# A decoder block on one Trainium2 core: three small pads shift the SBUF addresses of the matmul operands

## The chip, the core and the metric

The kernel runs on one core of one Trainium2 chip. The core has a matrix engine (TensorE: PE for the matmuls, PEld for the loads of their stationary operands), VectorE (DVE), ScalarE (ACT), GpSimd (POOL) and SyncE (SP), which here issues most of the DMAs. Tiles lie in the on-chip memory SBUF, which has 128 partitions; an address in this text is a byte address within a partition, the same in all of them. The metric is the device time of one execution in microseconds (us), the median of several.

## The reference

One layer of a decoder for 256 positions and 1024 channels, all float32:

```python
h = rmsnorm(x, ln1)
z = h @ w_in                      # q, k, v of three attentions, and three gates
o_a, o_b, o_c = moba_attention(..), forgetting_attention(..), sliding_window_sink_attention(..)
merged = sigmoid(ga) * (o_a @ w_pa) + sigmoid(gb) * (o_b @ w_pb) + sigmoid(gc) * (o_c @ w_pc)
x = x + merged @ w_o
h2 = rmsnorm(x, ln2)
u = causal_dwconv(h2 @ w_up, conv_w, conv_b)   # w_up: 1024 x 5632, three taps
a, b = split(u, 2)
return rmsnorm(x + (silu(a) * b) @ w_down, ln_f)   # w_down: 2816 x 1024
```

## The kernel before

**Numbers.** Every float32 product is made of three matmuls of a 4-byte type with fewer bits (float32r). Each operand is split into a high part and a rest: ScalarE copies the high part (`whi`, L110), VectorE subtracts it from the original (`wlo`, L117), and hi·hi, lo·hi and hi·lo are added up in PSUM. A matmul has a stationary operand of 128 x 128 and a moving operand of 128 partitions and up to 512 columns. Here both are read as 4-byte elements out of SBUF.

**Two kinds of product.** In a row product (`mm3`, L255 to L257) the activation is stationary and 512 columns of the weight move: the v and gate columns of `w_in`, the projections `w_pa`, `w_pb`, `w_pc` (`project`, activation `oT`), `w_o` (`wo_mm`, activation `mT` in the buffers named `hThi`, `hTlo`) and `w_down` (`down_mm`, activation `ah`, `al`). In a column product the weight is stationary and 256 positions of the activation move: the q and k columns of `w_in` (`qk_piece`, L406) and all of `w_up` (`up_mm`, L872). `w_up` has 44 pieces of 128 columns; each takes 24 matmuls (8 slices of the contraction, 3 parts each), 1056 in all. Its moving operand `h2T` lies in the buffers that the attention outputs had before, and so carries the names `oThi` and `oTlo` in the trace.

**Stages.** q, k, v, the attentions and the gates until about 151 us; the projections until 172 us; `w_o` until 198 us; then the channel mixer, 22 rounds of two `w_up` pieces and, in 18 of them, one `w_down` piece of 12 matmuls with 512 columns, until about 372 us; then the last four `w_down` pieces at once and the final norm.

**Weights.** `Weights` brings pieces of 512 KB through five `raw` buffers, splits them some pieces ahead of their use and hands out tiles of 4096 bytes a partition. Until `W.more` is set (L727) there are six `whi` and six `wlo` buffers in the pool `wpool`. From there on four more of each lie in the pool `ml`, and of every ten pieces in turn the first six take a buffer of `wpool`, the other four one of `ml` (`Weights.part`):

```python
if i >= first and (i - first) % (HL_BUFS + MORE_BUFS) >= HL_BUFS:
    return pool.tile([P, 1024], F32R, name=name, tag=name + "m", bufs=MORE_BUFS)
return self.pool.tile([P, 1024], F32R, name=name, tag=name, bufs=HL_BUFS)
```

**Addresses.** Pools lie one behind the other in SBUF, `const`, `wpool`, `act` and then, in the place that the attention's pool `attn` gives up, `ml`; inside a pool, tiles lie in the order in which they are first made. A tile that is made longer, or one that is made and never used, shifts all that follow it. All slices that matmuls read start at whole multiples of 256 bytes from the start of their tile, but for the v columns of `w_in` (780 floats to a piece). So the address of a tile modulo 256 is that of its slices.

Of the kernel before, what the change touches and what calls it, by code (L numbers as in the profile page):

```python
# [7 lines left out]
F32 = mybir.dt.float32  # L8
# [4 lines left out]
P = 128  # L13
# [127 lines left out]
def hybrid_kernel(ctx: ExitStack, tc: tile.TileContext, x, xT, ln_f, w_main, w_v1, w_v2, b_f, sinks,  # L141
# [4 lines left out]
    const = ctx.enter_context(tc.tile_pool(name="const", bufs=1))  # L146
    wpool = ctx.enter_context(tc.tile_pool(name="wpool", bufs=1))
    act = ctx.enter_context(tc.tile_pool(name="act", bufs=1))
# [36 lines left out]
    load_x(6, 8)  # L185
    W.load_to(4)
    cv = const.tile([P, 192], F32, name="cv")[:, :4 * 2 * NF + KD]
    ln2 = cv[:, 8 * NF:8 * NF + KD]
    W.load_to(6)
    for t in range(2):  # L190
# [68 lines left out]
    def small(shape, name, bufs=2):  # L259
        return act.tile([P] + shape, F32, name=name, tag=name, bufs=bufs)  # L260
# [269 lines left out]

    foxb = G[:, 1].rearrange("p t c -> p (t c)")[:, 0:4 * ROWS].rearrange("p (h c) -> p h c", h=4)
    lf, cum = small([8], "lf", 1), small([16], "cum", 1)[:, :8]

    def fox(logits):
        logits()
# [48 lines left out]


    oT = [act.tile([P, 8, S], F32R, name=n, tag=n, bufs=1) for n in ("oThi", "oTlo")]
    pair_state = {}

    def pair_of(p):
        if p < 2:  # L590
# [493 lines left out]
```

## Time and profile before

| what | us |
|---|---|
| median of 3 runs (394.5 to 395.8) | 395.03 |
| the profiled execution | 394.46 |
| its span, first to last instruction | 392.7 |
| PE busy | 382.7 |
| VectorE busy | 301.9 |
| ScalarE busy | 239.7 |

The profile is of one execution; 1.8 us of it lie outside the span. A matmul's own duration in the trace is no measure of what it costs, since matmuls overlap in the pipeline: one of 256 columns is listed with 0.28 us, and the next starts 0.11 to 0.12 us later. What counts is the time from one start to the next, called its step below. It is read from the starts of the first matmul of a run and of the first one behind it, divided by their number. The chain of waits gives the same: it lists runs of matmuls by length and number.

### The profile page before, as it was taken

Reading aid. Unit: us, or ns where it says so; the run is one execution under the profiler, and the core shown is the slowest. Engines: PE = TensorE matmul, PEld = TensorE weight load, DVE = VectorE, ACT = ScalarE, POOL = GpSimd, SP = SyncE. Lnnn points to the kernel's source line nnn. Section 1 sums busy time; section 2 is a strip of 40 time slices with the busy share of each in tenths; the row PEclk is TensorE's granted clock in tenths of the full one; section 3 lists DMA queues with packets and bytes.
Section 4 is the critical chain, followed back from the end, with each engine's and each line's share of the span. In section 5 each row is a group of like instructions: output and inputs, shape, how many; then the busy total and the mean of one; then the engine's idle time right before and its main releaser. Section 6 shows DMA issues by size and latency. Waiting matters only on the chain.

```text
span 392.7 us, 6636 instructions
## 1 busy us (share of the span) xinstructions
PE 382.7 (97%) x2464; PEld 346.9 (88%) x2464; DVE 301.9 (77%) x572; ACT 239.7 (61%) x431; POOL 15.3 (4%) x50
## 2 busy tenths in 40 slices
PE   7999999999999999999999999999999999999992
PEld 6899999888888888888899999999999999999982
DVE  4788998766777727967778999778887878888745
ACT  5875867657566696336587667456654656555433
POOL 4811000000000000000000000000000000000000
PEclk9999999999999999999999999999999999999998
DMA  7989764443543546443726667555565555463002
GB/s 195 402 308 344 271 213 164 161 141 116 173 120 103 165 150 221 154 160 118 259 107 221 205 214 236 198 187 189 164 213 174 204 169 204 166 212 107 2 1 108
DMA packets 21376, 70.88 MB, mean 180 GB/s; under 512 B 2504, under 2 KB 3413, under 8 KB 21344
## 3 DMA queue, kind: packets, MB, share of 16 engines
q1 hardware_dynamic: 20448, 68.05, 51.7%
q0 software_dynamic: 752, 2.18, 1.8%
q8 instruction: 19, 0.31, 0.3%
q10 hardware_dynamic: 144, 0.23, 0.2%
q14 instruction: 13, 0.11, 0.1%
HBM read 69.38 MB, written 1.07 MB: 179 GB/s over the span
## 4 chain that ended last, share of the span: by engine, by line
PE 96%; DMA 1%; DVE 1%; ACT 1%; SPq 1%; issue 0%; DVEq 0%
PE s L872 16%; PE acc L255 15%; PE acc L257 15%; PE acc L256 15%; PE pt L872 8%; PE o L872 8%; PE acc L406 7%; PE s L608 2%; PE pt L658 1%; DMA G<-in_xT 1%; PE pt L406 1%; PE o L406 1%; PE pt L661 1%; PE pt L645 1%; PE o L645 1%; PE s L313 0%
## 5 line engine op out<-in xcount | busy, mean ns | idle before, releaser
L117 DVE TENSOR_TENSOR wlo<-raw,whi 128x1024 fp32r<-128x1024 f32 (+4 forms) x131 | 150.5, 1162 | 14.1 <-ACT whi L110 13.8
L110 ACT ACTIVATE whi<-raw 128x1024 fp32r<-128x1024 f32 (+4 forms) x131 | 129.0, 1006 | 33.1 <-PE acc L256 21.7
L255 PE MATMUL acc<-whi,hThi 128*128 128x512 f32 (+2 forms) x160 | 62.4, 390 | 0.0
L257 PE MATMUL acc<-wlo,hThi 128*128 128x512 f32 (+2 forms) x160 | 60.1, 376 | 0.0
L256 PE MATMUL acc<-whi,hTlo 128*128 128x512 f32 (+2 forms) x160 | 59.9, 375 | 0.0
L872 PE MATMUL s<-oThi,whi 128*128 128x256 f32 x176 | 49.4, 281 | 0.0
L872 PE MATMUL s<-oThi,wlo 128*128 128x256 f32 x176 | 49.3, 281 | 0.0
L872 PE MATMUL s<-oTlo,whi 128*128 128x256 f32 x176 | 49.0, 281 | 0.0
L880 ACT ACTIVATE ya<-v,cv 128x256 f32<-128x256 f32 x22 | 13.3, 603 | 44.3 <-DVE v L877 44.3
L257 PEld LDWEIGHTS acc<-wlo,hThi 128*128 128x128 f32 x160 | 30.0, 188 | 5.4
L257 PE MATMUL acc<-wlo,ah 128*128 128x512 f32 (+1 forms) x88 | 34.2, 389 | 0.0
L255 PE MATMUL acc<-whi,ah 128*128 128x512 f32 (+1 forms) x88 | 34.1, 388 | 0.0
L256 PEld LDWEIGHTS acc<-whi,hTlo 128*128 128x128 f32 x160 | 30.2, 189 | 4.5 <-DVE hTlo L307 0.2
L256 PE MATMUL acc<-whi,al 128*128 128x512 f32 (+1 forms) x88 | 34.1, 388 | 0.0
L255 PEld LDWEIGHTS acc<-whi,hThi 128*128 128x128 f32 x160 | 30.1, 188 | 4.3
L872 PEld LDWEIGHTS s<-oThi,whi 128*128 128x128 f32 x176 | 33.1, 188 | 0.4
L872 PEld LDWEIGHTS s<-oThi,wlo 128*128 128x128 f32 x176 | 33.1, 188 | 0.4
L872 PEld LDWEIGHTS s<-oTlo,whi 128*128 128x128 f32 x176 | 32.9, 188 | 0.0
L872 PE MATMUL pt<-oThi,whi 128*128 128x256 f32 x88 | 24.8, 282 | 0.0
L872 PE MATMUL pt<-oThi,wlo 128*128 128x256 f32 x88 | 24.8, 282 | 0.0
L872 PE MATMUL o<-oThi,whi 128*128 128x256 f32 x88 | 24.8, 282 | 0.0
L872 PE MATMUL pt<-oTlo,whi 128*128 128x256 f32 x88 | 24.8, 282 | 0.0
(301 smaller groups left out, 801.5 us busy)
## 6 DMA issues: line engine op xcount, KB each, us to landing
raw<-in_w_main SPq DMA_DIRECT2D x115, 512.0 KB, 3.3
raw<-in_w_main SPq DMA_DIRECT2D x7, 256.0 KB, 6.1
raw<-in_w_v SPq DMA_DIRECT2D x4, 384.0 KB, 4.3
xt<-in_x SPq DMA_DIRECT2D x2, 512.0 KB, 6.9
G<-rowsd POOLq DMA_DIRECT2D x1, 1024.0 KB, 12.8
raw<-in_w_v SPq DMA_DIRECT2D x2, 390.0 KB, 6.6
G<-in_xT SPq DMA_DIRECT2D x3, 256.0 KB, 6.4
out_y<-xt SPq DMA_DIRECT2D x2, 288.0 KB, 2.2
```

Of the source, the lines that this page charges most:

```text
L110: self.nc.scalar.activation(self.parts[i][0][:, cs], self.raw[i][:, cs], AF.Copy)
L117: self.nc.vector.tensor_sub(lo[:, cs], self.raw[i][:, cs], hi[:, cs].bitcast(F32))
L255: nc.tensor.matmul(o, lh, rh, start=start, stop=False, **kw)
L256: nc.tensor.matmul(o, ll, rh, start=False, stop=False, **kw)
L257: nc.tensor.matmul(o, lh, rl, start=False, stop=stop, **kw)
L406: nc.tensor.matmul(o, w[:, kk, cs], hT[h][:, k, :], start=first, stop=last, skip_group_check=True)
L608: nc.tensor.matmul(sc, q[a][:, qi, qs], k[b][:, ki, :, 0:n], start=i == 0, stop=i == 2)
L645: nc.tensor.transpose(pts[e][:, i * P:(i + 1) * P], L[:, e, i * P:(i + 1) * P], ident)
L658: nc.tensor.matmul(o, v[a][:, vi, e, :], b[:, e, :], start=e == 0 and n == 0, stop=False, **kw)
L661: nc.tensor.matmul(o[:, P:S], v[2][:, vi, e, :], pT1[:, e, :], start=False, stop=e == 1, **kw)
L872: nc.tensor.matmul(u, w, h2T[h][:, k, :], start=k == 0 and i == 0, stop=k == KD - 1 and i == 2)
L880: nc.scalar.activation(y, v, AF.Identity, scale=w[2], bias=w[3])
```

## The change

Three tiles are added that nothing reads or writes, and a line that did nothing (`pair_state`) goes.

```diff
     cv = const.tile([P, 192], F32, name="cv")[:, :4 * 2 * NF + KD]
+    const.tile([P, 48], F32, name="pad0")
     ln2 = cv[:, 8 * NF:8 * NF + KD]
...
     lf, cum = small([8], "lf", 1), small([16], "cum", 1)[:, :8]
+    act.tile([P, 16], F32, name="pad1")
...
     oT = [act.tile([P, 8, S], F32R, name=n, tag=n, bufs=1) for n in ("oThi", "oTlo")]
-    pair_state = {}
+    act.tile([P, 32], F32, name="pad2")
```

The pads are 192, 64 and 128 bytes. All engines execute the same instructions in the same order with the same waits as before; only addresses differ. Modulo 256 they are, worked out from the order of the tiles (the distance is the moving operand's address less the stationary operand's, modulo 256):

| matmuls | number | columns | moving, stationary before | distance before | moving, stationary after | distance after |
|---|---|---|---|---|---|---|
| `w_up`, weight in `wpool` | 648 | 256 | 0, 128 | 128 | 0, 64 | 192 |
| `w_up`, weight in `ml` | 408 | 256 | 0, 192 | 64 | 0, 64 | 192 |
| `w_down`, weight in `wpool` | 159 | 512 | 128, 192 | 192 | 64, 64 | 0 |
| `w_down`, weight in `ml` | 93 | 512 | 192, 192 | 0 | 64, 64 | 0 |
| `w_down`, last columns, `wpool` | 18 | 256 | 128, 192 | 192 | 64, 64 | 0 |
| `w_down`, last columns, `ml` | 6 | 256 | 192, 192 | 0 | 64, 64 | 0 |
| `w_o`, weight in `ml` | 48 | 512 | 192, 128 | 64 | 64, 64 | 0 |
| `w_o`, weight in `wpool` | 48 | 512 | 128, 128 | 0 | 64, 64 | 0 |
| projections | 96 | 512 | 128, 0 | 128 | 64, 0 | 64 |
| q and k columns of `w_in` | 312 | 256 | 128, 128 | 0 | 64, 64 | 0 |
| gate and v columns of `w_in` | 384 | 260 to 512 | 128 to 160, 128 | 0 to 32 | 64 to 96, 64 | 0 to 32 |
| attention, products | 112 | 128 to 512 | 192, 192 | 0 | 64, 64 | 0 |
| attention, transposes | 48 | 128 | 128, 192 | 192 | 64, 64 | 0 |

## Rows read from the trace of the kernel before

**Rows 1.** The page: busy time, and the chain that ended last by engine and line
```profile
PE 382.7 (97%) x2464; PEld 346.9 (88%) x2464; DVE 301.9 (77%) x572; ACT 239.7 (61%) x431; POOL 15.3 (4%) x50
PE 96%; DMA 1%; DVE 1%; ACT 1%; SPq 1%; issue 0%; DVEq 0%
```

**Rows 2.** Waits of PE, whole span: who, for whom, us in total, times, longest
```profile
PE pt L406 <- ACT whi L110: 1.4, 2, 1.1
PE s L199 <- DVE warm L196: 1.1, 1, 1.1
PE pt L406 <- DVE wlo L117: 0.4, 2, 0.2
```

**Rows 3.** Chain in order of time, `w_up` alone: start, us, engine, PSUM tile, line, matmuls
```profile
198.59 1.42 PE s L872 x12
...
205.16 2.88 PE pt L872 x24
...
219.37 2.83 PE pt L872 x24
...
253.16 2.88 PE pt L872 x24
...
284.28 2.85 PE pt L872 x24
...
368.94 2.87 PE o L872 x24
```

**Rows 4.** Timeline of PE, last columns of `w_down`: start, us, engine, line, operation, out<-in
```profile
382.81 0.28 PE L255 MATMUL acc<-whi,ah 128*128 128x256 f32 x1
...
383.16 0.28 PE L255 MATMUL acc<-whi,ah 128*128 128x256 f32 x1
...
383.84 0.28 PE L255 MATMUL acc<-whi,ah 128*128 128x256 f32 x1
```

**Rows 5.** Chain in order of time: q and k columns, transposes, attention times v
```profile
52.29 6.47 PE acc L406 x54
58.76 0.33 PE pt L645 x3
...
63.92 0.71 PE pt L658 x6
...
179.72 0.87 PE s L313 x8
```

**Rows 6.** Timeline of PE: two `w_down` pieces, each with the first matmul behind it
```profile
241.83 0.39 PE L255 MATMUL acc<-whi,ah 128*128 128x512 f32 x1
...
244.58 0.28 PE L872 MATMUL s<-oThi,whi 128*128 128x256 f32 x1
...
267.22 0.39 PE L255 MATMUL acc<-whi,ah 128*128 128x512 f32 x1
...
270.01 0.28 PE L872 MATMUL pt<-oThi,whi 128*128 128x256 f32 x1
```

**Rows 7.** Timeline of PE: first projection piece, pieces of `w_o`, starts alone matter
```profile
150.79 0.40 PE L255 MATMUL acc<-whi,oThi 128*128 128x512 f32 x1
...
153.58 0.39 PE L255 MATMUL acc<-whi,oThi 128*128 128x512 f32 x1
...
176.12 0.39 PE L255 MATMUL acc<-whi,hThi 128*128 128x512 f32 x1
...
178.87 0.39 PE L255 MATMUL acc<-whi,hThi 128*128 128x512 f32 x1
...
183.19 0.40 PE L255 MATMUL acc<-whi,hThi 128*128 128x512 f32 x1
...
188.02 0.40 PE L255 MATMUL acc<-whi,hThi 128*128 128x512 f32 x1
```

**Rows 8.** Windows of the mixer, last `w_down` pieces: us, busy by engine, clock, DMA, GB/s
```profile
216.00:372.00 156.00, 156.00 (x1124) 147.12 (x1123) 130.91 (x217) 93.33 (x137) 0.00 (x0) 1.00 0.54 179
371.65:378.64 6.99, 6.99 (x33) 5.64 (x31) 2.25 (x5) 2.61 (x4) 0.00 (x0) 1.00 0.00 0
```

## The prediction

> **What bounds the kernel now.** First the busy shares and the chain: PE is busy for 97% of the span, and 96% of the chain that ended last is PE [rows 1]. Then the waits of PE: three kinds, 2.9 us together, all on the first products (L199, L406) [rows 2]. From the projections on nobody makes PE wait, so a nanosecond of step saved is a nanosecond of time, and what is to be asked is what a step consists of. In the window of the channel mixer PE is busy without a gap at full clock (1.00), VectorE for 130.9 of 156 us, ScalarE for 93.3, the DMA engines for 54% [rows 8].
>
> Third, the chain's runs of `w_up`. It lists all 1056 matmuls in 35 runs that add up to 125.2 us, a mean step of 118.6 ns; first and last stand in [rows 3]. At 2.4 GHz 256 columns take 106.7 ns, so 12 ns of each step are something else. The runs of 24 between them show what the reader is to see: the same instruction, with the same shape and the same clock, takes 2.83 us in one run, 2.85 in another, 2.88 in a third [rows 3]. These values come back with the buffers. The run at 219.37 has its weight in `ml`, distance 64, and every run with such a weight takes 2.83, which is 117.9 ns a step. The runs at 205.16, 253.16 and 284.28 have theirs in `wpool`, distance 128: 2.85 (118.8 ns) or 2.88 (120.0 ns), never less. DMAs, VectorE and ScalarE work differently beside each of these runs, and the values do not move; the addresses are what is left.
>
> **What the distance does, from rows.** Two things make the table of distances usable.
> First, shifting both operands alike changes nothing. With 512 columns at distance 0, a `w_down` piece at (192, 192) takes 2.75 us for its 12 matmuls, 241.83 to 244.58 [rows 6], and a `w_o` piece at (128, 128) takes 2.75 us for 12, 176.12 to 178.87 [rows 7]. I take it that this holds for other distances and for a shift of 128 too; that is the main choice of this forecast.
> Second, for 256 columns all four distances stand in the trace. Distance 128: 118.8 or 120.0 ns. Distance 64: 117.9 ns. Distance 0: 6.47 us for 54 matmuls of q and k, 119.8 ns, and 0.71 for 6 in the attention, 118.3 ns [rows 5]. Distance 192: only the last columns of `w_down`. There the first three steps take 0.35 us, 382.81 to 383.16, and the next six 0.68, to 383.84: 113.3 ns [rows 4]. A second run of the same kind follows it and reads alike. This is where the change puts all of `w_up`.
>
> **The change part by part.** The instructions, their order and their waits stay, so every term is a number of matmuls times a change of step.
>
> 1. `w_up`, 1056 matmuls, to distance 192. Now 125.2 us [rows 3]. Then 1056 x 113.3 ns = 119.7 us, and some 10 ns at the start of each of the 22 rounds until the step has settled (0.35 against 3 x 0.1133 [rows 4]), 0.2 us. Together 119.9: **-5.3 us**. Bounds: at 120.0 ns, the slowest settled step of 256 columns in the rows, 126.7 us, +1.5; nothing in the trace settles below 113.3, so that is the other end.
> 2. `w_down`, 159 matmuls of 512 columns from distance 192 to 0. The piece from 267.22 to 270.01 lies at 192: 2.79 us for 12, 232.5 ns; that from 241.83 at 0: 2.75, 229.2 ns [rows 6]. 159 x 3.3 ns = **-0.5 us**. The 93 at distance 0 stay.
> 3. `w_o`, 48 matmuls from distance 64 to 0: 183.19 to 188.02 is 21 matmuls in 4.83 us, 230.0 ns, against 229.2: 48 x 0.8 ns, below **-0.1 us**.
> 4. Projections, 96 matmuls from distance 128 to 64. First piece: 12 in 2.79 us (150.79 to 153.58), 232.5 ns; at distance 64 the nearest row is the `w_o` one, 230.0 ns [rows 7]. 96 x 2.5 ns = -0.2; I take **-0.1 us**, since the gain per matmul hangs on a single stretch.
> 5. The last columns of `w_down`, 18 matmuls of 256 from distance 192 to 0: from some 114.4 ns (nine steps in 1.03 us [rows 4]) to the 118.3 ns of a short run at distance 0 [rows 5]: **+0.1 us**.
> 6. The attention's products, q, k, v and gates keep their distances: 0. The attention's 48 transposes of 128 columns go from 192 to 0; three of them take 0.33 us now, and eight transposes of another line, at distance 0 already, 0.87, which is the same 0.11 a step [rows 5]: 0. The pads cost no instruction, and the line that goes cost none.
>
> Sum: -5.3 - 0.5 - 0.1 - 0.1 + 0.1 = **-5.9 us**. The profiled execution goes from 394.46 to 388.6 us, its span from 392.7 to 386.8. It lies 0.57 us below the median of the runs, so the median goes from 395.03 to **389.1 us**, -1.5%.
>
> What is late next: a round of the mixer (48 matmuls of `w_up`, 12 of `w_down`) gets some 0.3 us shorter out of 8.5. VectorE's 130.9 us then stand against some 150.5 instead of 156, 87% instead of 84%. It works up to eight pieces ahead of PE, so that a late piece costs nothing unless it is late on average; at 87% it isn't. DMA goes from 54% to 56%.
>
> **A rule against the change.** The rows say that the step depends on where the two operands of neighbouring matmuls lie. The Trainium skill, "TensorE: Matmul & The Clock Gate", Part 2 (step 1 of what each phase is for), says that the engine has two independent SBUF read ports and that loading the next weights takes no read bandwidth from the running matmul; its "SBUF — State Buffer", Who interferes with whom, says that PE never waits on anyone. By these two the step would be the same at every address, the sum 0 and the time 395.0. The trace disagrees: 2.83 and 2.88 us for the same 24 matmuls [rows 3].
>
> **The rivals.**
> - *Addresses don't matter*, and the runs differ for another reason. For it: no field of the profile shows an address, and the 113.3 ns come from a stretch without DMA. Against it: the three values follow the buffers over 156 us in which DMA and VectorE vary. Time 395.0. Chance 0.05.
> - *The settled step is a matter of history.* At distance 128 some runs settle at 118.8 and others at 120.0 ns [rows 3], so one distance can have two settled steps, and after a `w_down` piece `w_up` may fall into a slower one at distance 192 too. If half of the runs stay at 117.9, the step of distance 64, term 1 is 528 x 4.6 ns = 2.4 us smaller: 391.5. If the distance is not what counts but the address, and all stay at 117.9, term 1 is -0.7: 393.7. Chances 0.10 and 0.04.
> - *VectorE becomes late.* The mixer's gain is then cut to what VectorE can follow; with 13% of slack I see at most a third given back: 391. Chance 0.03.
> - *Distance 192 is a bad one (the other side).* With 512 columns it is the slowest for `w_down`: 232.5 against 229.2 [rows 6]. The last columns of `w_down` could owe their 113.3 ns to the quiet memory at the end. If the 3.3 ns hold for 256 columns too, on top of the 119.8 at distance 0, `w_up` costs 1056 x 123.1 = 130.0 us, +4.8, and with the other terms the time is 399.2. It decides from a mean step of 119.1 ns on, where term 1 eats the 0.6 us of the rest. Against it: the first 30 of the last `w_down` matmuls, at distance 192 and with no DMA beside them, take 6.99 us ([rows 8]; three of the 33 counted had started before), 233.0 ns a step, as much as the 232.5 in the mixer; the quiet memory changes nothing there. Chance 0.05.
>
> **How the numbers follow.** The forecast, 389.1, has 0.73; its own spread is the runs' half us and a fifth of term 1, 388.0 to 390.2. For 8 in 10 the range must take in the half-settled case and VectorE's: 387.7 to 391.8, with 0.73 x 0.97 + 0.13 = 0.84. A measurement of this kernel can tell about 0.3% from no change, 1.2 us: faster than 393.8 are the forecast, the mixed cases and half of the 393.7 case, 0.88; same 0.07; slower 0.05.
>
> **What would show it.** In the changed kernel's chain the `w_up` runs of 24 must read 2.72 to 2.74 us, all alike, no matter which buffer; runs of 2.83 or more mean the address and not the distance, a mix means history. `w_down` pieces must read 2.75 or less each, those at the very end too. q, k, attention and gates must end at the same moment as now, about 150.8 us; if they move, shifting both operands alike is not neutral, and the main choice is wrong. VectorE's and ScalarE's durations must not move; new waits of PE for `wlo` would mean VectorE.

## The result and the profile after

| | before | after |
|---|---|---|
| median, us | 394.89 (5 runs, 394.5 to 395.8) | 392.43 (5 runs, 392.0 to 393.3) |
| the profiled execution | 394.46 | 392.43 |
| its span | 392.7 | 390.7 |

The ratio of after to before is 0.9937, with a 95% interval of 0.9919 to 0.9955: 0.6% faster, where 1.5% was forecast. 392.43 lies above the upper end of the range, 391.8.

What bounds the kernel has not changed. The page's busy shares and its chain by engine read as before [rows 1], and so do PE's waits (for whom; us in total, times, longest): they all lie on the first products [rows 2].

```profile
PE 379.8 (97%) x2464; PEld 345.7 (88%) x2464; DVE 301.6 (77%) x572; ACT 239.5 (61%) x431; POOL 15.7 (4%) x50
...
PE 96%; DMA 1%; DVE 1%; SPq 0%; ACT 0%; issue 0%; DVEq 0%
```

```profile
PE pt L407 <- ACT whi L110: 2.6, 2, 2.4
PE s L200 <- DVE warm L197: 1.1, 1, 1.1
PE pt L407 <- DVE wlo L117: 0.2, 1, 0.2
```

The first weights let PE wait 1.4 us in all before and 2.6 here. In the profiles of the kernels below, all with the same instructions up to there, it is between nothing (e8) and 2.1, so it varies from execution to execution.

Where the 2.0 us between the two profiled executions lie, with each matmul counted from its start to the start of the next one:

| stretch | matmuls | before, us | after, us | difference | forecast |
|---|---|---|---|---|---|
| up to the first projection | | 150.8 | 151.6 | +0.8 | 0 |
| `w_up` | 1056 | 125.4 | 124.1 | -1.3 | -5.3 |
| `w_down`, 512 columns | 252 | 58.3 | 57.1 | -1.2 | -0.5 |
| projections | 96 | 22.4 | 22.1 | -0.3 | -0.1 |
| `w_o` | 96 | 22.7 | 22.5 | -0.2 | below -0.1 |
| last columns of `w_down` (23 steps) | 24 | 2.6 | 2.75 | +0.1 | +0.1 |

Most of the first line is the loading of the first pieces: the run of 66 matmuls of q and k, the first long one, starts at 26.11 before and at 26.74 after, and between 26.17 and 27.84 in the kernels below. So 4.0 us of the forecast are missing in the line of `w_up`. The chain in order of time (start, us, engine, PSUM tile, line, number of matmuls) shows it; here and in the chains below the rows of `w_up` alone stand, and "..." marks rows of `w_up` left out:

```profile
200.75 4.18 PE s L874 x36
205.37 2.73 PE pt L874 x24
208.11 2.72 PE o L874 x24
210.83 5.44 PE s L874 x48
219.00 2.83 PE pt L874 x24
...
227.38 5.65 PE s L874 x48
...
367.11 2.83 PE o L874 x24
```

The first two of the 22 rounds have no `w_down` piece; the first piece follows the third round. From 205.37 to 216.27, the second and third round, 24 matmuls take 2.72 us, 113.3 ns a step, as forecast. Then comes the first `w_down` piece, and from 219.00 to the end each run of 24 takes 2.83 (48 take 5.65): 117.8 ns, whatever buffer the weight lies in. The addresses in the two stretches are the same, moving 0 and stationary 64 modulo 256. The difference of 4.5 ns on some 910 matmuls is 4.1 us, all that is missing.

The timeline of PE (start, us, engine, line, operation, out<-in) shows a `w_down` piece and the first `w_up` matmuls behind it:

```profile
224.49 0.39 PE L256 MATMUL acc<-whi,ah 128*128 128x512 f32 x1
...
226.99 0.39 PE L258 MATMUL acc<-wlo,ah 128*128 128x512 f32 x1
227.21 0.28 PE L874 MATMUL s<-oThi,whi 128*128 128x256 f32 x1
227.33 0.28 PE L874 MATMUL s<-oThi,wlo 128*128 128x256 f32 x1
```

Twelve matmuls from 224.49 to 227.21 are 2.72 us, 226.7 ns each. The faster pieces of before took 2.75 [rows 6]. Behind the piece the first `w_up` step is 0.12, and there is no transient: PE enters the step of 117.8 ns at once and stays in it.

### The profile page after: what moved, and what is told of

Its sections match the earlier page's. It is cut to its first block, busy times and chain, and to the rows that moved or that the text cites. A ratio compares the mean times of both kernels' runs of the same rounds, so it can differ in the third digit from the quotient of the medians.

```text
span 390.7 us, 6636 instructions
## 1 busy us (share of the span) xinstructions
PE 379.8 (97%) x2464; PEld 345.7 (88%) x2464; DVE 301.6 (77%) x572; ACT 239.5 (61%) x431; POOL 15.7 (4%) x50
## 4 chain that ended last, share of the span: by engine, by line
PE 96%; DMA 1%; DVE 1%; SPq 0%; ACT 0%; issue 0%; DVEq 0%
PE s L874 16%; PE acc L256 15%; PE acc L258 15%; PE acc L257 15%; PE pt L874 8%; PE o L874 8%; PE acc L407 7%; PE s L610 2%; PE pt L660 1%; DMA raw<-in_w_main 1%; PE pt L407 1%; PE o L407 1%; PE pt L663 1%; PE o L647 1%; PE pt L647 1%; PE s L314 0%
```

## The experiments

Two theories were open. **History**: distance 192 has two settled steps, 113.3 and 117.8 ns, and the moment at which PE comes out of the matmuls ahead, against the rhythm of the loads, decides which one it falls into. **Address**: something other than the distance, such as the address itself or what DMA and the other engines do meanwhile, makes the 117.8. Edits below are made to the changed kernel unless said otherwise. All medians and ratios are against the kernel before on the same chip. Sums for `w_up` are those of the chain, where before has 125.2 [rows 3] and after 123.9 us.

**1. Another `w_down`, the same `w_up`.** Two kernels move only `ah` and `al`, so that `w_down` lies at distance 192 or at 64. `w_up` keeps all its addresses.

```diff
+        if j == 0:
+            ml.tile([P, 16], F32, name="pad3")    # e1; [P, 48] in e2
```

> As the changed kernel, with one more pad of 64 bytes ahead of the tiles ah and al, so that they lie at 128: w_down goes from distance 0 to 192, w_up stays at 192 and is entered from a w_down piece at 192, as the last columns of w_down were in the kernel before. History (distance 192 has two settled steps of 256 columns, 113.3 and 117.7 ns, and the phase at the entry decides): w_up settles at 113.3 in all rounds, 1000 x 4.4 ns = 4.4 us less; w_down pays 252 x 6.6 ns = 1.7 us (233.3 against 226.7 ns); 389.7 us. Load (113.3 ns need the quiet of the first round and of the end, VectorE and DMA beside it make it 117.7): w_up stays at 117.7, 394.1 us.

> As the changed kernel, with a pad of 192 bytes ahead of ah and al, so that they lie at 0: w_down at distance 64, w_up at 192. History: w_down at 229.0 to 233.3 ns, +0.6 to +1.7 us; w_up has one of its two values, the same in every round after the first: 388.6 to 389.7 us if it is 113.3, 393 to 394 if it is 117.7. Load: 393 to 394 us.

e1 (`w_down` at 192) took 391.92 us, ratio 0.9932 (0.9908 to 0.9956). Its chain goes back and forth: a round at 2.83 for 24, the next at 5.46 for 48, which is 113.7 ns with its first steps, and so on to the end. `w_up` sums to 122.4 us. So neither of the two expected times came: history had been expected to make all rounds alike. The step changes over in all 17 rounds that have a `w_down` piece ahead of them. The two later rounds without one (274.41 and 330.18) keep the step of the round before them.

```profile
218.64 2.83 PE pt L874 x24
...
227.09 5.46 PE s L874 x48
235.34 2.83 PE pt L874 x24
...
274.41 5.66 PE s L874 x48
282.87 2.74 PE pt L874 x24
```

e2 (`w_down` at 64) took 390.18 us, 0.9867 (0.9841 to 0.9893). All its rounds from the second on are fast, and `w_up` sums to 120.4:

```profile
219.79 2.75 PE pt L874 x24
...
228.00 5.47 PE s L874 x48
```

The `w_up` instructions, their addresses and what DMA and VectorE do beside them are those of after; only the matmuls ahead of them were moved. That speaks for history. The alternation of e1 fits no rule by address: what a round takes over from the round before it counts as well as the piece between them. The price: `w_down` takes 232.9 ns a step at distance 192 and 229.0 at 64, against 226.7 at 0.

**2. The same addresses, another moment.** e3 puts a small matmul, with 32 output rows and 32 columns, ahead of every round of `w_up` but the first. e4 cuts the last three matmuls of each `w_down` piece into two of 256 columns each; e8 does so from the second piece on, and e11 cuts only the very last matmul of each piece from the second on, 17 of 252. No address moves.

```diff
+        if c == 0:                                                       # e3
+            nc.tensor.matmul(u[0:32, 0:32], h2T[0][:, 0, 0:32], h2T[0][:, 0, 0:32], start=True, stop=True)
...
-                down_mm(j, t, half * 512, half * 512 + 512, parts)
+                if t and half:                                           # e4; j and t and half in e8
+                    down_mm(j, t, 512, 768, parts)
+                    down_mm(j, t, 768, D, parts)
...
+                    for c in (0, 256):                                   # e11: the last matmul alone
+                        nc.tensor.matmul(zo[1][1][:, c:c + 256], ah[:, ts],
+                                         lo[:, 512 + c:768 + c], start=False, stop=False, ...)
```

> As the changed kernel, with one matmul of 32 rows of output and 32 columns, whose result is overwritten, ahead of the first matmul of every round of w_up but the first; no address changes. It costs 0.05 to 0.12 us each, 1 to 2.5 us. History: it shifts the phase in which w_up starts; if that lands it on the 113.3 ns step, -4.4 us and 389 to 390.5 us, else 393.4 to 395 us, and which of the two is the same in every round. Load: w_up at 117.7 ns, 393.4 to 395 us.

> As the changed kernel, with the last three matmuls of each w_down piece in the mixer cut into two of 256 columns each; addresses and results as they are. Cost: 18 x 3 x some 13 ns = 0.7 us. History: w_up is entered from 256 columns at distance 0 and not from 512, another phase: 388.8 us if it settles at 113.3 ns, 393.1 if at 117.7, alike in all rounds that follow a w_down piece. Load: 393.1 us.

> As e4_last_quarter_split, but the first w_down piece is left whole, so that the output is complete. History: 389.7 us as there, w_up at 113.3 ns in every round that follows a split piece, 117.7 in the one that follows the whole piece. Load: 392.4 us or more.

> As the changed kernel, with only the very last matmul of each w_down piece in the mixer (but the first piece) cut into two of 256 columns; 17 of 252. Cost 17 x 13 ns = 0.2 us. History: a shift of phase of that size is enough to change the settled step or it isn't, alike in all rounds that follow a cut piece: 113.3 ns and 388.8 us, or 117.7 and 392.6. Were the step a matter of addresses alone, 392.6 us.

e3 took 392.02 us, 0.9927 (0.9903 to 0.9951). That lies between the two expected ranges. The added matmul costs some 0.1 us at each round (the first run of 24 reads 2.84 instead of 2.75 or less), about half of what the faster rounds gain. Behind it `w_up` runs at 113.3 ns in each round that follows a `w_down` piece. Three rounds follow another one directly, and there the same small matmul changes the step over: behind a round at 117.8 it leads to 113.3 (210.65, 5.55 = 0.1 + 5.45), behind one at 113.3 to 117.8 (274.37 and 330.00; 5.75 = 0.1 + 5.65).

```profile
204.89 2.92 PE pt L874 x24
...
210.65 5.55 PE s L874 x48
218.96 2.84 PE pt L874 x24
...
274.37 5.75 PE s L874 x48
```

e4 took 389.67 us, 0.9861 (0.9843 to 0.9878), with 113.3 ns in all rounds behind a `w_down` piece. In e4 the output is not complete: the first piece starts the sums, and with it cut a part of its contribution is missing; the work done is the same. e8, where the first piece stays whole and the output is complete, took 389.49, 0.9856 (0.9826 to 0.9886). Its chain has both steps side by side: the round behind the whole piece, then the rounds behind cut ones.

```profile
218.44 2.83 PE pt L878 x24
...
226.84 5.46 PE s L878 x48
235.07 2.74 PE pt L878 x24
```

e11, with one matmul in fifteen cut, took 390.51, 0.9863 (0.9832 to 0.9894), and reads alike:

```profile
205.97 2.83 PE pt L886 x24
...
220.02 2.83 PE pt L886 x24
...
228.40 5.46 PE s L886 x48
236.59 2.74 PE pt L886 x24
```

The timeline of e11 behind a cut shows how the faster step is reached. After the two halves of 0.23 us together come four steps of 121, 122, 116 and 114 ns (0.12, 0.12 and so on in the rows), and only then 113.3:

```profile
228.00 0.40 PE L876 MATMUL acc<-wlo,ah 128*128 128x256 f32 x2
228.23 0.29 PE L886 MATMUL s<-oThi,whi 128*128 128x256 f32 x1
228.35 0.28 PE L886 MATMUL s<-oThi,wlo 128*128 128x256 f32 x1
```

That settles it between the two theories: with no address changed, a different last matmul ahead of a round sets the step of the 48 that follow, in all 16 rounds that have a cut piece ahead of them. PE comes to the first cut piece from a round at 117.8, as it does to the same piece in after, and leaves it at 113.3. The round behind the uncut piece of the same execution stays as it was, and the two later rounds with no piece ahead keep the faster step. The times of e2, e4 and e11 lie 0.5 to 1.7 us above what history had expected for the faster step. In e11, 0.7 us of that lie ahead of the first projection, and 0.4 us are the second and third round, which ran at 117.8.

The instructions ahead are not all of it. Up to the first `w_down` piece, the changed kernel, e4, e8 and e11 execute the same instructions at the same addresses. The second and third round take 113.3 ns in after and e8, but 117.8 in e4 and e11 (2.83 for 24 at 205.97 above, against 2.73 at 205.37 in after). So one sequence can take either step from one execution to the next, on the same chip too: e2, the same up to there but for the place of `ah` and `al`, takes 113.3, and e4, which ran on its chip, 117.8.

**3. Is it the distance or the address?** e6 takes the first pad away, which puts all operands behind it 192 bytes lower, 64 higher modulo 256 (not 64 lower, as its expectation has it), and keeps all distances. e5 takes the third away (then `w_up` with its weight in `ml` lies at distance 64), e10 the second (then 648 `w_up` matmuls lie at 128 and 408 at 192).

```diff
-    const.tile([P, 48], F32, name="pad0")     # e6
-    act.tile([P, 32], F32, name="pad2")       # e5
-    act.tile([P, 16], F32, name="pad1")       # e10
```

> The change without its first pad: every address from the weights on is 64 bytes lower modulo 256 than in the changed kernel, all distances are the same. Distance theory: step by step the changed kernel, w_up at 113.3 ns in the first round and 117.8 after, w_down at 226.7, 392.4 us. Address theory (what counts is that the moving operand of w_up lies at 0 and the weights at 64): w_up at another step, 118.8 to 120 as at the old addresses, 393.5 to 395 us.

> The change without its third pad: the pool ml lies at 192, so 648 matmuls of w_up are at distance 192 and 408 at 64, and 159 of w_down at 128, 93 at 0. History: 117.8 ns for the 408 as in the kernel before; the 648 at 113.3 or at 117.7 ns by the phase in which each run is entered, maybe not the same in all rounds; 391.1 us if all are fast, 394 if none is. That is no better than the whole change or better than it, although the pad was part of it.

> The change without its second pad: h2T lies at 192 and the pool ml at 0, so that w_up has 648 matmuls at distance 128 and 408 at 192, w_down 159 at 64 and 93 at 0. Distance and history: the 648 at 118.5 to 120 ns as in the kernel before, the 408 at 113.3 (as after w_down at 64 in e2_act_at_0) where they follow such a piece, else 117.7; -0.5 to -2.5 us in w_up, -0.6 in w_down, 391.7 to 393.8 us.

e6 took 392.40 us, 0.9922 (0.99 to 0.9944). Its chain is that of after run for run, 0.6 us later, as it already is at the first long run of q and k (27.37 against 26.74):

```profile
205.99 2.73 PE pt L873 x24
...
211.44 5.44 PE s L873 x48
219.62 2.83 PE pt L873 x24
```

`w_up` sums to 123.94 us in both, `w_down` to 57.13 in both. So for this kernel a shift of all operands by 64 doesn't matter while the distances stay, which was the main choice of the forecast.

e5 took 392.88 us, 0.9939 (0.9917 to 0.996). Rounds at distance 64 read 2.83 throughout. Of the 11 rounds at 192 behind a `w_down` piece five are fast (5.45 for 48 at 227.65 and at 261.12, for instance), and six are slow (2.83 for 24 at 235.87). There is an order in it: behind a `w_down` piece at distance 128 a round is fast where the round before it ran at 117.8, and slow where that ran at 113.3, in eight of eight; behind one at distance 0 it is slow, in three of three.

```profile
227.65 5.45 PE s L873 x48
235.87 2.83 PE pt L873 x24
```

e10 took 396.22, 1.0021 (1.0002 to 1.0041), as slow as before or slower: 2.88 at distance 128 behind a `w_down` piece at 64 (2.84 or 2.85 behind one at 0), and at distance 192 not one round behind a `w_down` piece is fast. The first and the last row below are at 192, the other two at 128.

```profile
221.20 2.83 PE pt L873 x24
...
229.62 5.76 PE s L873 x48
238.14 2.88 PE pt L873 x24
...
246.64 5.65 PE s L873 x48
```

I had priced e10 between after and before, with the 113.3 for a part of the rounds at 192; that was wrong. Which of the two steps a round gets cannot be read from the distances alone: with the same 192, all rounds, half or none are fast, by what stands ahead.

**4. What meets what.** e9 hands every `w_up` matmul one column of its weight 128 times over as the stationary operand, so that the load no longer walks through 512 bytes of each partition. If two walks through SBUF that meet were all there is to it, one step should be left.

```diff
-            nc.tensor.matmul(u, w, h2T[h][:, k, :], start=k == 0 and i == 0,
+            nc.tensor.matmul(u, w[:, 0:1].to_broadcast([P, P]), h2T[h][:, k, :], start=k == 0 and i == 0,
```

> As the changed kernel, but every stationary operand of w_up is the first column of its weight slice repeated 128 times, so the product is not the reference's; the load of the stationary operand then reads one address instead of walking through 512 bytes. Meeting theory (the step above 109 ns comes from the moving read and the load of the next weights meeting at addresses): no dependence on history is left, one step in all rounds, between 109 and 113.3 ns, w_up 115 to 120 us instead of 124.3, 384 to 388 us. Rival (the moving read alone makes the step): 117.8 ns after the first round as in the changed kernel, 392.4 us.

e9 took 389.84 us (2 runs), 0.9858 (0.9817 to 0.99). Two steps are left, but others: 120.0 ns in the second and third round (2.88 for 24), 113.3 from the first `w_down` piece on, just the reverse of after.

```profile
204.82 2.88 PE pt L874 x24
...
210.58 5.76 PE s L874 x48
219.09 2.73 PE pt L874 x24
```

Neither expectation held. The two steps don't need the walk, and what the load and the moving operand contend for stays open.

**5. The other products, and the best of it.** e7 puts the q and k columns at distance 192 as well, and the gate and v columns and `w_o` at 64, with `w_down` at 64. e12 has the same addresses but `w_down` at 0, and e11's cut.

```diff
-    const.tile([P, 48], F32, name="pad0")
...
+    act.tile([P, 48], F32, name="pad4")       # ahead of hT
...
-    act.tile([P, 16], F32, name="pad1")
+    act.tile([P, 32], F32, name="pad1")
...
+            ml.tile([P, 48], F32, name="pad3")    # e7 alone, ahead of ah
```

> As e2_act_at_0 (w_up at distance 192 entered from w_down at 64), and the tiles hT moved as well, so that the q and k columns are at distance 192 instead of 0 and gates, v columns and w_o at 64 instead of 0. History: the 312 matmuls of q and k at 113.3 or 117.7 ns instead of 119.8, of which the ones before 26 us wait for DMA: -0.5 to -1.6 us; 480 matmuls of 512 columns or fewer between 0.2 us less and 1.5 us more; against e2 between -1.8 and +1.0 us, 388.4 to 391.2 us.

> The distances of e7_all_columns_192 but w_down back at 0, with the cut of e11_one_cut: q, k and w_up at distance 192, w_down at 226.7 ns instead of 229.2 (-0.6 us against e7, +0.2 for the cuts). History: 388.8 us if the cut leads w_up to 113.3 ns, 392.5 if not, as in e11_one_cut.

e7 took 389.25 us, 0.9831 (0.9805 to 0.9858); e12 took 388.62, 0.9828 (0.9806 to 0.985), the fastest of all, with an interval that it shares with e7. In e12's chain the first 66 matmuls of q and k run at 113.5 ns; in after they took 7.90 us. The later ones, which follow row products, run at 117.8 (6.36 us for 54) against 119.8 [rows 5]. So q and k have two steps at distance 192 as well.

```profile
26.25 7.49 PE acc L407 x66
...
51.82 6.36 PE acc L407 x54
```

The row products that went from distance 0 to 64 (gates, v and `w_o`, 480 matmuls) take 104.7 us in e7 and 104.6 in after: hardly a difference, though `w_down` lost 2.3 ns a step by the same move in e2. In e12 PE waits for nobody from the projections on either, as in all the kernels above; its waits are the three kinds of after, 1.9 us together.

## Why the prediction was right or wrong

**Right: what bounds the kernel, and the sign.** A step saved is time saved: PE waits for nobody after the first products, before, after and in the fastest variant. The small terms came out at -0.3 (projections), -0.2 (`w_o`) and +0.1 us (last columns), against -0.1, below -0.1 and +0.1.

**Right: the main choice.** Shifting both operands alike is neutral; e6 shows it to 0.01 us in `w_up` and `w_down`, for a shift by 64. The rival that addresses don't matter falls by e6 and e10 together: the same three pads less one give 392.4 or 396.2, by which distances are left. With that, the rule that I weighed from the Trainium skill ("TensorE: Matmul & The Clock Gate", Part 2, and "SBUF — State Buffer", Who interferes with whom), by which the step would be the same at every address, is contradicted by a second pair of kernels. What the first of the two pages says of the ports themselves is not tested: e9 leaves open what contends.

**Wrong: term 1, `w_up` at distance 192 settles at 113.3 ns.** The step that failed is the one from "nothing at distance 192 in the trace reads otherwise" to "distance 192 means 113.3". The row for it [rows 4] was of one place, the last columns of `w_down`, with one history. Distance 192 has two settled steps. In the changed kernel the matmuls behind a `w_down` piece, at distance 0, fall into the slower one, 117.8 ns, and they did so in every round behind one. Term 1 came to -1.3 us instead of -5.3, just what the rounds ahead of the first `w_down` piece and the 1 to 2 ns a step from 118.8 or 120.0 down to 117.8 bring.

**The rival that was right, and its price.** History was among the rivals, with 0.10 for half of the runs in the slower step, at 391.5, and 0.04 for all of them, at 393.7, but the latter only as a matter of the address. All runs slow *by history* had no line of its own. The evidence was in the rows: at distance 128, runs settle at 118.8 and at 120.0 [rows 3]. The prediction said of these values that they come back with the buffers, but both are of weights in `wpool`. The trace of before has more: from the first `w_down` piece on it has three rounds at 120.0, and they are the three at distance 128 behind a `w_down` piece at distance 0 (weight in `ml`, worked out from the order of the pieces). The eight behind one at 192 settle at 118.8 or a little less.

```profile
253.16 2.88 PE pt L872 x24
...
309.61 5.75 PE s L872 x48
...
366.06 2.88 PE pt L872 x24
```

The change puts every `w_down` piece at distance 0. That was a sign, not a rule: in e10 it is the rounds behind distance 64 that read 120.0. If one distance has two steps in the trace of before, then a step read in one place is one of an unknown number, and whether the rounds share a fate is not left to chance: they repeat the same instructions, and in all kernels but e1 and e5 the rounds at one distance behind `w_down` pieces at one distance entered alike. The case "all rounds slow" belonged in the sum, with a chance not far from the forecast's. The prediction's own sign misled too: runs of 2.83 or more were to mean the address, a mix history. After reads 2.83 in every round behind a `w_down` piece, and e6 and e11 show that this is history.

**Wrong in size: term 2, `w_down`.** -1.2 us instead of -0.5. I took 229.2 ns for distance 0 from a piece of before; in after the pieces run at 226.7 from their first matmul. The 159 that moved gained 5.8 ns each (-0.9 us), and the 93 that kept their distance gained 2.6 as well (-0.2); they are entered from another `w_up`, which is the likely reason. Of the values at the same distance 0 I had taken a mean over a piece that had not settled, again one place read as the distance's step, with the sign turned.

**VectorE late, and distance 192 a bad one.** Both fall. No new wait of PE appears, not even in e12 with the mixer 5 us shorter than before; VectorE's 1216 ns and ScalarE's 1045 for a split of 128x1024 are unchanged within 1 ns. With 256 columns distance 192 reads 113.3 or 117.8, never more than the 120.0 of distance 0 (e9, with another stationary operand, apart), in spite of the 232.9 that it costs with 512 columns (e1).

**Two readings of the rows.** The chain of before lists the 1056 matmuls in 34 runs, not 35, and the runs at distance 128 read down to 2.84. Neither changes the sum.

**The end of the first half.** "q, k, attention and gates must end at the same moment" read 151.6 instead of 150.8. Of this, 0.6 us were there before the first long run of q and k, and that start moves by 1.7 us between kernels with the same addresses there (26.17 in e8, 27.84 in e10); the sums for gates and v are 82.1 us before and 82.2 after. I count it as scatter of the start, not as a cost of the shift, as e6 and e11 with their other starts suggest.

## What to carry to other kernels

When PE never waits, read the step from start to start, sort it by operand buffer, and look at the addresses modulo 256 of the two operands: in this kernel the products with 256 moving columns were fastest at distance 192 and those with 512 at distance 0. A step read in one place is not yet the step of that distance elsewhere: look for a second settled value at any distance, and if there is one, give the case that all rounds take the slower step a price and a chance of its own: here the rounds shared a fate in most kernels, and in e1 and e5 about half of them were fast. Where a loop has fallen into the slower step, changing the last instruction ahead of it may be enough: cutting 17 of 252 matmuls in two took another 2 us here (392.4 to 390.5; ratio 0.9937 to 0.9863).

## What the runs showed of the hardware

The following settled steps (ns, from start to start, at full granted clock) were seen in this case for 4-byte operands, by the distance of moving less stationary address modulo 256:

| columns moving | distance 0 | 64 | 128 | 192 |
|---|---|---|---|---|
| 256 | 120.0 | 117.8, or 113.3 | 118.6 to 118.8, or 120.0 | 113.3, or 117.8 |
| 512 | 226.7 | 229.0 | 232.4 | 232.9 |

The 113.3 at distance 64 is that of the last columns of `w_down` in e2; `w_up` at 64 settled at 117.8 in all its rounds, before and in e5. So a step of 113.3 is not the property of distance 192 alone, and whether `w_up` at 64 could be brought to it was not tried.

I had not expected that the same `w_up` instructions at the same addresses can run for 150 us in either of two steps, nor that it is as repeatable as it is: each of the 16 rounds of e11 behind a cut piece begins with the same 121, 122, 116 and 114 ns. Nor does the change-over need another instruction. In after, the 36 matmuls from 200.50 reach 113 to 114 ns after some steps and pass to 118 at about 202.88. That is where the order of the three parts changes, and where the first matmul starts that reads what VectorE finished writing into `oTlo` 0.16 us before:

```profile
202.65 0.28 PE L874 MATMUL s<-oThi,whi 128*128 128x256 f32 x1
202.76 0.28 PE L874 MATMUL s<-oThi,wlo 128*128 128x256 f32 x1
202.88 0.64 PE L874 MATMUL s<-oTlo,whi 128*128 128x256 f32 x4
203.35 0.28 PE L874 MATMUL s<-oThi,whi 128*128 128x256 f32 x1
203.47 0.28 PE L874 MATMUL s<-oThi,wlo 128*128 128x256 f32 x1
```

e4 and e11 have the same instructions and addresses there, and from 178.5 us on (times of after) all their steps had been equal to those of after within 2 ns. They too have a step of 122 ns at this place, but then go back to 113. At the next break, four matmuls of 128 columns at 204.77 in after, each changes over: after to 113.3, e4 and e11 to 117.8. What differs at the first place is a few nanoseconds, and with them the step that follows. The profile lists no wait of PE here, so whether the matmul waited for VectorE for some nanoseconds is open.

What the moment of entry shifts, the load against the running matmul or something else, no field of the trace shows, and e9 doesn't tell it. That it is a phase between the two reads is my reading, not shown. Shown is that with all addresses kept another matmul ahead changes the step (e4, e8, e11), and that the same matmuls ahead can lead to either (after against e4 and e11).
